# Nine edits of stage borders in a two-layer diffusion block on one core

## The chip, the cores and the metric

The kernel runs on one core of one Trainium2 chip. The metric is the device time of one execution in microseconds, taken as the median of several runs. An execution has one time of its own, and its profile has a span, from the first to the last instruction.

## The reference

Two transformer layers over 1024 latent tokens and 256 context tokens of width 1024, all in float32. Each layer is attention, an output projection, a layer norm, a gated feed-forward network with a 3-wide convolution, and a second layer norm. A conditioning vector gives shift, scale and gate for each half ("modulation").

```python
for i in range(2):
    sh1, sc1, g1, sh2, sc2, g2 = adaln(c, w_ada, b_ada)          # 6 x 1024 for the tokens
    csh1, csc1, cg1, csh2, csc2, cg2 = adaln(c_ctx, w_ada, b_ada)  # the same for the context
    h, hc = x * (1 + sc1) + sh1, xc * (1 + csc1) + csh1
    y, yc = mixer_i(h, hc)                    # attention, then @ w_out (1024 x 1024)
    x = layer_norm(ALPHA * x + g1 * y, ln1_g, ln1_b)
    h = x * (1 + sc2) + sh2
    x = layer_norm(ALPHA * x + g2 * conv_ffn(h), ln2_g, ln2_b)   # up: 1024 x 5632, down: 2816 x 1024
    # layer 0 does the same to the context; layer 1 has no use for it after the mixer,
    # so of its context modulation only csh1 and csc1 are read
return x
```

## The kernel before

Every float32 operand of a product is split in a high and a low part (`split_hi`, a cast; `split_lo`, a subtraction), and a product is three matmuls (`three`). Any of VectorE (DVE), ScalarE (ACT) and GpSimd (POOL) can do a split; the code says which. Tokens are worked on in chunks: chunk 0 and 1 are 512 tokens each, chunk 2 the 256 of the context. Activations lie feature-major, so a layer norm transposes on TensorE (PE), norms the rows and transposes back.

The tail of a layer (`layer_tail`) has these stages in program order:

- **Projection** (`proj`): eight output blocks of 128 features, first for chunk 0 (layer 0: chunks 0 and 2), then again for chunk 1. `load_wo` loads one 512 KB block of `w_out` and splits it on POOL, with the low part of odd blocks on DVE. The two first blocks are loaded ahead; each later one in its own turn. The steps of the first layer norm (`ln1`) of chunks 2 and 0 are woven in the second pass.
- **LN1 of chunk 1** (`ln1(1)`): four tiles of 128 tokens through `normalise`, eight feature blocks through `back_rows`, and then 20 operand tiles of the Strassen-like up product (sums of quarters, each split). The first products of the up stage (`HEAD` = 2 feature blocks in layer 0, 3 in layer 1; P1 and P2 of each) need chunk 0 alone and run between.
- **Up** (`up_step`): 22 feature blocks of seven products. In layer 0 one step of `next_modulation` follows each product: a DVE multiply-add over `w_ada` of layer 1. A piece (`ada_piece`) is eight such steps, four 512 KB loads, a split and a pair of matmuls.
- **Down** (`down_items`): three or four groups of feature-block pairs, seven products each; weights and activations are split as they come.
- **End**: layer 0 goes on to `layer1_head` (second layer norm, the latent projections, then per head group `up_q` and `up_kv`); layer 1 to `finish` (the last products per chunk, the last layer norm, the output).

Attention has a hand-written order with due times. Around it the Tile framework orders the instructions of each engine by program order and readiness, and a tile waits for a free slot of its tag. DMAs are issued in order on the SP queue, a few on POOL's (the first head of layer 1's attention, L2240) and ACT's. Slots of layer 0's tail: 7 of 2 KB ("r"), 32 of 2 KB ("b"), 11 of 4 KB ("c4", where `w_out` raw and split, the rows `z`, `x` and `w_ada` all go); layer 1: 8, 36, 12. PSUM has eight banks; the P1 bank of a feature block stays open until its P4.

Of the kernel before, what the change touches and what calls it, by code (L numbers as in the profile page):

```python
# [392 lines left out]
def tile_hybrid_block(ctx: ExitStack, tc: tile.TileContext, *aps):  # L393
# [182 lines left out]

    def ada_finish(l, ps, first=16, ends=(48, 48)):

        nc.tensor.transpose(ps[:, 0:96], arow, ident[0:96, 0:96])
        for c in range(2):  # L580
            a, b = first, ends[c]
            if a == b:
                continue
            nc.vector.tensor_add(
                mods[l][:, c, a:b], ps[:, 48 * c + a : 48 * c + b], vec_a[:, 16 + 48 * l + a : 16 + 48 * l + b]
            )
            for i in (1, 4):
                if a <= 8 * i < b:
                    nc.vector.tensor_scalar(mod(l, c, i), mod(l, c, i), 1.0, None, op0=ALU.add)

# [661 lines left out]
    def layer_tail(l, after, kept=None):  # L1252
# [48 lines left out]

        wo = []

        def load_wo(ci, m):
            first = ci == 0 and m == 0
            wo.append(
                load_w(
                    cols(A[f"l{l}_w_out"][:, m * P : (m + 1) * P]), f"o{l}_{ci}_{m}",
                    eng=("act" if first else "pool", "dve" if m % 2 or first else "pool"),
                )  # L1310
            )

        def proj(cis):
            for m in range(KB):
                if not wo:
                    load_wo(cis[0], m)
                wh, wl = wo.pop(0)
                for ci in cis:
                    c0, cn = chunks[ci]
                    yh, yl = ytiles[ci]  # L1320
                    ps = ps1(f"pso{l}_{ci}_{m}")
                    mm_acc(
                        ps[:, :cn],
                        [p3 for k in range(KB) for p3 in three(wh[:, k, :], wl[:, k, :], yh[:, k, :], yl[:, k, :])],
                    )
                    gate = mod(l, ci // 2, 2, m)
                    if l == 0:
                        nc.scalar.activation(acc[ci][:, m, :], ps[:, :cn], AF.Copy, scale=gate)
                    else:
                        xr = tl("xr", (512,), f"xr{l}_{ci}_{m}")  # L1330
                        nc.sync.dma_start(xr[:, :cn], x2_scr[m * P : (m + 1) * P, c0 : c0 + cn])
                        nc.vector.scalar_tensor_tensor(
                            acc[ci][:, m, :], ps[:, :cn], gate, xr[:, :cn], op0=ALU.mult, op1=ALU.add
                        )
                yield

        def normaliser(acc, pool, tl, ps1):
            def normalise(ci, j, name, residual=None, tag="c5", later=None):
# [19 lines left out]
                if later is not None:  # L1358
                    later.append((mv, rs))
                elif j % 2:  # L1360
                    nc.vector.tensor_scalar(rs[:, 1:2], mv[:, 0:1], rs[:, 0:1], -1.0, op0=ALU.mult, op1=ALU.mult)
                    nc.scalar.activation(z, z, AF.Identity, bias=rs[:, 1:2], scale=rs[:, 0:1])
                else:
                    nc.vector.tensor_scalar(z, z, mv[:, 0:1], rs[:, 0:1], op0=ALU.subtract, op1=ALU.mult)
# [4 lines left out]
        def back_rows(ci, zs, name, scales, residual, tl, ps1, order=range(KB)):  # L1369
# [3 lines left out]
            for m in order:  # L1373
                pb = ps1(f"pb{name}_{ci}_{m}")
                for j, z in enumerate(zs):
                    nc.tensor.transpose(pb[:, j * P : (j + 1) * P], z[:, m * P : (m + 1) * P], ident)
                tmp = tl("aa", (512,), f"tmp{name}_{ci}_{m}")[:, :cn]
                nc.vector.tensor_scalar(
                    tmp, pb[:, :cn], scales[0][:, m : m + 1], scales[1][:, m : m + 1], op0=ALU.mult, op1=ALU.add,
                )  # L1380
                if residual is not None:
                    residual(m, pb[:, :cn])
                yield m, tmp
# [67 lines left out]

        HEAD = 2 if l == 0 else 3
        lo, hi = slice(0, 512), slice(512, 1024)
# [131 lines left out]
        def next_modulation():  # L1585

            late = None
            for q, c in [(q, c) for c in range(2) for q in range(4)]:
                sums, rows = ada_piece(1, q, (c,), ps1, tl)
# [7 lines left out]
            run(late)  # L1597
            ada_finish(1, ps1("ps_af1"), 0, (16, 16))


        GROUPS = [(0, 1), (2, 3, 4), (5, 6, 7), (8, 9)] if l == 0 else [(0, 1, 2), (3, 4, 5, 6), (7, 8, 9)]
        def down_items():
# [31 lines left out]
            for i, (gi, js, what) in enumerate(steps):  # L1634
# [15 lines left out]
                if what != "A21":  # L1650
                    for j in js:
                        r = got.pop((i, j))
                        xh, xl = (tl("b", (512,), f"a{what}{s}_{l}_{j}", F32R) for s in "hl")
                        split_hi(xh, r, "act")
                        split_lo(xl, r, xh, "dve" if what in ("P1", "P3") else "pool")
                        xs.append((xh, xl))
# [59 lines left out]
        for m in range(2):  # L1716
            load_wo(0, m)
        if l == 0:
# [13 lines left out]
        for i in range(2 * HEAD):  # L1732
            step()
            for _ in range(4):
                next(rows, None)
# [151 lines left out]
        def back(ci, zs, name, scales, dst, residual):  # L1887
            for m, h in back_rows(ci, zs, name, scales, residual, tl, ps1):
# [6 lines left out]
             "feature_tile": feature_tile, "normalise": normaliser(acc, AC, tl, ps1), "back": back,  # L1895
             "load_w": load_w, "last_down": last_down,
             "tl_ada": lambda tag, shape, name, dt=F32: tlT("c4" if tag == "aw" else "r", shape, name, dt)}
        after(K)
# [6 lines left out]
    def layer1_head(K):  # L1905
# [96 lines left out]
        def rotate(x, tok, n, name):  # L2002
# [186 lines left out]
        run(norms[1])  # L2189
        def rest_of_modulation():  # L2190
            late = iter(())
            for q in range(4, 12):
                sums, rows = ada_piece(1, q, (0,), ps1, K["tl_ada"])
                for _ in sums:
                    next(late, None)
                    yield
                run(late)
                late = rows
            run(late)
            ada_finish(1, ps1("ps_af1"), 16, (48, 16))  # L2200

        mods_late = rest_of_modulation()

        def also(steps, n):
            for x in steps:
                for _ in range(n):
                    next(mods_late, None)
                yield x
# [54 lines left out]
    def finish(K):  # L2263
# [106 lines left out]
```

## Time and profile before

| | |
|---|---|
| median of 3 runs | 3573.13 us (3570.94 to 3577.04) |
| the profiled execution | 3575.87 us |
| its span | 3574.1 us |
| mean granted clock of PE | 0.965 |
| busy | PE 93%, weight loads 79%, DVE 68%, ACT 48%, POOL 44% |

The profiled execution's time is 1.8 us above its span and 2.7 us above the median. PE is the busiest engine; where it is idle, time is lost if the PE work behind it can't be made up.

### The profile page before, as it was taken

To read this page: it belongs to the slowest core of one execution; us is meant where nothing else is said; L and a number is where in the kernel's file an instruction comes from. 1 tells how busy PE (TensorE), PEld (TensorE's weight loads), DVE (VectorE), ACT (ScalarE), POOL (GpSimd) and SP (SyncE) were. 2 spreads that over 40 slices of the span, in tenths; PEclk is the share of its full clock that TensorE was granted. 3 is DMA by queue.
4 is the path that set the end of the run, shared out by engine and by line. 5 is a ranking of instruction groups with operands and counts; after the bars stand their busy time and mean duration, and the time that the engine had idled before them with its cause. 6 is when DMAs were issued, how large, how long until landed. Compare 5 with 4: busy or idle time off the path is not lost.

```text
span 3574.1 us, 52193 instructions
## 1 busy us (share of the span) xinstructions
PE 3307.3 (93%) x18683; PEld 2836.0 (79%) x18683; DVE 2447.3 (68%) x3777; ACT 1709.7 (48%) x3255; POOL 1584.3 (44%) x1794
## 2 busy tenths in 40 slices
PE   7998898988789999999999987999999889999997
PEld 5988787877668888888877776999998768888775
DVE  6687787873598766675655764777775387777665
ACT  4222677762354433443335323777775254444342
POOL 4533787652300000057734522888887300000985
PEclk9999999999899999999999988999999999999998
DMA  6367411574344422263323588232333323334541
GB/s 213 113 206 217 112 44 45 160 190 135 124 133 156 141 86 88 77 230 113 98 73 105 178 304 252 53 82 64 81 75 90 106 96 104 98 109 144 189 133 71
DMA packets 383744, 454.50 MB, mean 127 GB/s; under 512 B 27956, under 2 KB 255196, under 8 KB 383484
## 3 DMA queue, kind: packets, MB, share of 16 engines
q1 hardware_dynamic: 370284, 424.55, 39.2%
q10 hardware_dynamic: 11424, 18.94, 1.5%
q0 software_dynamic: 1776, 7.67, 0.6%
q8 instruction: 147, 2.41, 0.3%
q14 instruction: 113, 0.93, 0.1%
HBM read 328.78 MB, written 122.22 MB: 126 GB/s over the span
## 4 chain that ended last, share of the span: by engine, by line
PE 70%; DVE 9%; POOL 9%; issue 5%; DMA 3%; ACT 2%; SPq 0%; ACTq 0%; POOLq 0%; DVEq 0%
PE pu L1448 22%; PE pd_P L1778 10%; PE psum L194 7%; PE psum L335 5%; PE pso L417 5%; PE psum L304 5%; PE px L1522 3%; POOL p L264 3%; PE pw L417 2%; PE psq L417 2%; PE px L1778 2%; PE ps_f L417 2%; DVE aa L552 2%; PE ps_tu L417 1%; POOL pl L312 1%
## 5 line engine op out<-in xcount | busy, mean ns | idle before, releaser
L194 PE MATMUL psum<-k,q 96*128 96x512 f32 (+1 forms) x1152 | 272.8, 374 | 15.1 <-DMA k<-kr_scr 12.4
L412 POOL TENSOR_TENSOR dP<-dr,dP 128x512 fp32r<-128x512 f32 x40 | 57.0, 1445 | 454.2 <-ACT dP L404 450.5
L194 PEld LDWEIGHTS psum<-k,q 96*128 96x128 f32 x1152 | 196.8, 192 | 43.8 <-issue 12.8
L264 POOL TENSOR_SCALAR p_m<-p_m,st_m 128x640 f32<-128x640 f32 x256 | 202.6, 804 | 12.6
L552 DVE SCALAR_TENSOR_TENSOR aa<-aw,silu_late,aa 128x512 f32<-128x512 f32 x224 | 196.1, 905 | 15.4 <-DMA aw<-in_l_w_ada_dram 13.9
L320 DVE TENSOR_TENSOR pl_m<-psum,ph_m 128x512 fp32r<-128x512 f32 x256 | 175.0, 684 | 38.0 <-ACT ph_m L314 37.0
L304 PE MATMUL psum<-ident,p_m 128*128 128x128 f32 x1280 | 193.1, 273 | 2.5 <-DVE pl_m L320 2.2
L251 ACT ACTIVATE p_m<-psum,st_m 128x1024 f32<-128x1024 f32 (+2 forms) x192 | 187.0, 984 | 17.3 <-DVE st_m L244 16.4
L314 ACT CAST ph_m<-psum 128x512 fp32r<-128x512 f32 x256 | 151.0, 591 | 87.5 <-PE psum L304 44.1
L412 POOL TENSOR_TENSOR aal<-aa,aah 128x512 fp32r<-128x512 f32 x32 | 50.3, 1583 | 307.5 <-ACT aah L404 282.5
L412 POOL TENSOR_TENSOR aP2l<-ar_P,aP2h 128x512 fp32r<-128x512 f32 x20 | 28.7, 1450 | 354.0 <-ACT aP2h L404 346.9
L1770 DVE SCALAR_TENSOR_TENSOR acd<-pd_P,mods,acd 128x512 f32<-128x512 f32 x196 | 140.4, 742 | 54.9 <-PE pd_P L1778 49.9
L335 PE MATMUL psum<-ph_m,v 128*128 128x256 f32 x640 | 175.3, 301 | 0.6 <-DVE y_m L353 0.6
L335 PE MATMUL psum<-ph,v 128*128 128x256 f32 (+1 forms) x512 | 150.2, 316 | 23.0 <-DVE y L368 11.9
L241 DVE TENSOR_REDUCE st_m<-psum 128x1 f32<-128x1024 f32 (+1 forms) x128 | 105.6, 825 | 88.5 <-PE psum L194 88.5
L320 DVE TENSOR_TENSOR pl<-psum,ph 128x512 fp32r<-128x512 f32 (+1 forms) x224 | 144.7, 647 | 30.6 <-ACT ph L314 27.5
L335 PE MATMUL psum<-pl_m,v 128*128 128x256 f32 x640 | 164.1, 282 | 0.0
L304 PE MATMUL psum<-ident,p 128*128 128x128 f32 x960 | 151.7, 278 | 10.5 <-ACT p_c L118 4.3
L264 POOL TENSOR_SCALAR p<-p,st 128x640 f32<-128x640 f32 x192 | 152.9, 805 | 12.6
L314 ACT CAST ph<-psum 128x512 fp32r<-128x512 f32 (+1 forms) x224 | 122.9, 557 | 66.3 <-PE psum L304 59.3
L304 PEld LDWEIGHTS psum<-ident,p_m 128*128 128x128 f32 x1280 | 149.0, 141 | 4.0 <-DVE pl_m L320 3.1
L304 PEld LDWEIGHTS psum<-ident,p 128*128 128x128 f32 x960 | 110.3, 141 | 29.0 <-DVE pl L320 8.0
(599 smaller groups left out, 11406.5 us busy)
## 6 DMA issues: line engine op xcount, KB each, us to landing
aw<-in_l_w_ada_dram SPq DMA_DIRECT2D x96, 512.0 KB
ur<-in_l_w_up_dram SPq DMA_DIRECT2D x176, 256.0 KB
ar_P<-a_scr SPq DMA_DIRECT2D x140, 256.0 KB
a_scr<-a_t SPq DMA_DIRECT2D x80, 256.0 KB
dr<-in_l_w_down_dram SPq DMA_DIRECT2D x80, 256.0 KB
fr_o<-in_l_w_out_dram SPq DMA_DIRECT2D x32, 512.0 KB
a_scr<-cv SPq DMA_DIRECT2D x60, 256.0 KB
v<-v_scr SPq DMA_DIRECT2D x17, 640.0 KB
```

Source lines behind the costliest of these rows:

```text
L194: nc.tensor.matmul(u["s"][bank][:, c:e], q[:, qc], ks, start=pi == 0, stop=pi == len(u["passes"]) - 1)
L251: nc.scalar.activation(pt, src if bias is None else pt, AF.Exp, bias=st[:, j, 2:3], scale=1.0 if bias is None else -1.0, accum_out=st[:, j ...
L264: nc.gpsimd.tensor_scalar(pt, pt, st[:, j, 7:8], 0.0, op0=ALU.mult, op1=ALU.add)
L304: nc.tensor.transpose(tp[:, off + bi * P : off + bi * P + P], pts[j][:, c : c + P], ident)
L314: nc.scalar.copy(ph[:, :w], tp[:, :w])
L320: nc.vector.tensor_tensor(pl[:, :w], tps[g][:, :w], ph[:, :w].bitcast(F32), ALU.subtract)
L335: nc.tensor.matmul(u["av"][:, q0 : q0 + bw], u["v"][:, kt, :], m[:, off : off + bw], start=first and part == 0, stop=last and part == 1, s ...
L417: nc.tensor.matmul(ps, s, m, start=i == 0, stop=i == n - 1)
L552: nc.vector.scalar_tensor_tensor(accs[c], w, sck, accs[c], op0=ALU.mult, op1=ALU.add)
L1448: nc.tensor.matmul(ps, st, mv, start=start and i == 0, stop=i == len(pairs) - 1, skip_group_check=True)
L1770: nc.vector.scalar_tensor_tensor(acc[ci][:, m, :], src, mod(l, ci // 2, 5, m), acc[ci][:, m, :], op0=ALU.mult, op1=ALU.add)
L1778: nc.tensor.matmul(ps, st, mv, start=start and i == 0, stop=i == len(pairs) - 1, skip_group_check=True)
```

## The change

Nine edits:

1. `load_wo` loads a block in two 256 KB halves (tag "r"), two blocks ahead of its use through both passes; high parts on ACT, low parts on DVE, except that in the second pass the first half's go to POOL.
2. In LN1 of chunk 1 (both layers) all four tiles are normed on ACT, and `back_rows` makes its scaled copy on ACT.
3. `HEAD` of layer 1 is 4 rather than 3, with three steps of `ln1(1)` after each product rather than four.
4. The whole of layer 1's modulation (16 pieces) is made in the up stage of layer 0. Before, 8 pieces were made there and 8 in `layer1_head` (`rest_of_modulation`).
5. In `down_items` the low parts of odd pairs' activations go to DVE.
6. The pool of the first head of layer 1's attention (`pf`) is opened before that of the other heads (`pk`), so it lies at another address.
7. `finish` does chunk 1 in halves of 256 tokens.
8. The rotation's temporary takes a slot of "acc512".
9. The order of the last head group's `up_q` and `up_kv` is "bbbabaa" rather than "bbababa".

```diff
-        def load_wo(ci, m):
-            first = ci == 0 and m == 0
-            wo.append(
-                load_w(
-                    cols(A[f"l{l}_w_out"][:, m * P : (m + 1) * P]), f"o{l}_{ci}_{m}",
-                    eng=("act" if first else "pool", "dve" if m % 2 or first else "pool"),
-                )
-            )
+        out_blocks = iter([(p, m) for p in range(2) for m in range(KB)])
+
+        def load_wo():
+            p, m = next(out_blocks, (None, None))
+            if p is None:
+                return
+            wh, wl = (tl("fw", (KB, P), f"fo{s}{l}_{p}_{m}", F32R) for s in "hl")
+            for half in range(2):
+                ks = slice(4 * half, 4 * half + 4)
+                raw = tl("r", (4, P), f"ro{l}_{p}_{m}_{half}")
+                nc.sync.dma_start(
+                    raw,
+                    A[f"l{l}_w_out"][half * 512 : half * 512 + 512, m * P : (m + 1) * P].rearrange("(k p) c -> p k c", p=P),
+                )
+                split_hi(wh[:, ks], raw, "act")
+                split_lo(wl[:, ks], raw, wh[:, ks], "dve" if p == 0 or half else "pool")
+            wo.append((wh, wl))
...
-                if not wo:
-                    load_wo(cis[0], m)
                 wh, wl = wo.pop(0)
+                load_wo()
...
-                elif j % 2:
+                elif j % 2 or ci == 1 and name[0] == "a":
                     nc.vector.tensor_scalar(rs[:, 1:2], mv[:, 0:1], rs[:, 0:1], -1.0, op0=ALU.mult, op1=ALU.mult)
                     nc.scalar.activation(z, z, AF.Identity, bias=rs[:, 1:2], scale=rs[:, 0:1])
...
+                if ci == 1 and name[0] == "a":
+                    nc.scalar.activation(
+                        tmp, pb[:, :cn], AF.Identity, bias=scales[1][:, m : m + 1], scale=scales[0][:, m : m + 1]
+                    )
+                else:
...
-        HEAD = 2 if l == 0 else 3
+        HEAD = 2 if l == 0 else 4
...
-            for q, c in [(q, c) for c in range(2) for q in range(4)]:
+            for q, c in [(q % 12, q // 12) for q in range(16)]:
...
-                        split_lo(xl, r, xh, "dve" if what in ("P1", "P3") else "pool")
+                        split_lo(xl, r, xh, "dve" if what in ("P1", "P3") or j % 2 else "pool")
...
-            for _ in range(4):
+            for _ in range(4 if l == 0 else 3):
                 next(rows, None)
...
-            t = tl("aa", (512,), f"rt_{name}")[:n]
+            t = T.tile([P, 512], F32, name=f"rt_{name}", tag="acc512", bufs=16)[:n]
...
-        weave(also(up_q(0), 4), also(kv, 4), "")
+        weave(up_q(0), kv, "")
         for g in range(1, 4):
-            weave(also(up_q(g), 3), also(up_kv(g), 3), "babababa" if g < 3 else "bbababa")
-        run(mods_late)
+            weave(up_q(g), up_kv(g), "babababa" if g < 3 else "bbbabaa")
...
+        pf = es.enter_context(wait_pool("att1f", "right"))
         pk = es.enter_context(wait_pool("att1k", "right"))
-        pf = es.enter_context(wait_pool("att1f", "right"))
...
-        for ci, o, n in ((0, 0, 512), (1, 0, 512)):
+        for ci, o, n in ((0, 0, 512), (1, 0, 256), (1, 256, 256)):
```

`ada_finish` is fitted to the pieces' new place and does the same additions.

## Rows read from the trace of the kernel before

**Rows 1.** Windows: busy us (instructions) of each engine, PE clock, DMA share, GB/s.

```profile
887.40:971.40 84.00, 59.74 (x265) 46.91 (x264) 44.31 (x73) 26.04 (x45) 26.60 (x23) 0.80 0.34 105
...
971.40:1023.10 51.70, 34.87 (x198) 28.52 (x196) 46.96 (x83) 25.59 (x41) 3.47 (x5) 0.89 0.23 84
...
1030.00:1182.00 152.00, 152.00 (x798) 128.41 (x796) 132.36 (x194) 69.84 (x115) 11.13 (x6) 1.00 0.55 173
...
1182.00:1260.00 78.00, 76.35 (x402) 64.37 (x401) 54.33 (x84) 31.69 (x53) 4.69 (x2) 1.00 0.34 105
...
1260.00:1445.00 185.00, 185.00 (x976) 157.56 (x976) 117.31 (x175) 74.09 (x121) 0.00 (x0) 1.00 0.27 88
...
2054.00:2199.00 145.00, 128.82 (x633) 107.93 (x634) 92.14 (x143) 45.47 (x96) 38.39 (x44) 0.91 0.80 283
...
2757.00:2857.00 100.00, 87.80 (x389) 71.26 (x389) 39.31 (x56) 18.78 (x30) 39.84 (x28) 0.91 0.41 122
...
2868.00:2909.30 41.30, 29.32 (x128) 21.66 (x128) 39.42 (x67) 26.30 (x43) 1.92 (x2) 0.92 0.26 86
...
3305.00:3340.00 35.00, 27.24 (x108) 21.28 (x107) 21.24 (x21) 14.29 (x25) 35.00 (x24) 0.85 0.47 149
...
3551.70:3574.10 22.40, 4.30 (x30) 2.94 (x28) 18.06 (x24) 6.70 (x10) 10.42 (x6) 0.72 0.23 94
```

**Rows 2.** Waits in 887.4 to 971.4: us in total, times, longest.

```profile
PE pso L417 <- POOL fh_o L408: 15.6, 3, 7.6
...
PE pba L1376 <- DVE za L1364: 6.1, 2, 3.2
```

**Rows 3.** Chain of work that ended last: start us, us, what.

```profile
906.78 5.63 PE pso L417 x24
...
957.36 1.31 PE pba L1376 x12
...
1050.00 2.73 PE pu L1448 x12
...
2186.82 0.46 PE ps_a L417 x2
```

**Rows 4.** Timeline of layer 1's LN1 of chunk 1, ACT and DVE.

```profile
2868.46 0.62 ACT L404 CAST wP<-ur_00h 128x512 fp32r<-128x512 f32 x1
...
2868.98 1.25 ACT L1362 ACTIVATE za<-za,rs_a 128x1024 f32<-128x1024 f32 x1
...
2869.93 0.68 DVE L412 TENSOR_TENSOR wP<-ur_00h,wP 128x512 fp32r<-128x512 f32 x1
...
2873.03 0.81 DVE L1378 TENSOR_SCALAR tmpa<-pba,der 128x512 f32<-128x512 f32 x1 [1.16 <-PE pba L1376]
...
2873.88 0.78 ACT L1408 ACTIVATE rs<-pba,der 128x512 f32<-128x512 f32 x1 [1.27 <-DVE tmpa L1378]
```

**Rows 5.** Waits of PE in 2800 to 2910.

```profile
PE pso L417 <- POOL fh_o L408: 10.5, 2, 5.3
```

**Rows 6.** Tile aa and aal: min/median/max ns, first and last start.

```profile
L552 DVE SCALAR_TENSOR_TENSOR aa<-aw,silu_late,aa x224: 732/745/1831, 206.2 to 2180.4; 128x512 f32<-128x512 f32 x112
...
L412 POOL TENSOR_TENSOR aal<-aa,aah x32: 1267/1372/3400, 229.0 to 2181.9; 128x512 fp32r<-128x512 f32 x32
```

**Rows 7.** Waits of PE in 2070 to 2230.

```profile
PE psum L194 <- DMA k<-kr_scr: 12.4, 1, 12.4
...
PE psq L417 <- ACT uqh L404: 11.0, 1, 11.0
```

**Rows 8.** POOL's timeline where layer 1's attention begins.

```profile
2199.04 0.70 POOL L2240 DMA_DIRECT2D q<-q_scr  x1 [11.85 <-PE psq L417]
```

**Rows 9.** Waits of PE in 3305 to 3515.

```profile
PE pd_P L1778 <- POOL aP6l L412: 11.3, 5, 6.5
```

**Rows 10.** Groups by line in 3305 to 3515: count, busy us, mean ns, idle before.

```profile
L412 POOL TENSOR_TENSOR aP6l<-ar_P,aP6h 128x512 fp32r<-128x512 f32 x10 | 14.8, 1497 | 0.1
...
L412 DVE TENSOR_TENSOR aP3l<-ar_P,aP3h 128x512 fp32r<-128x512 f32 x10 | 13.4, 1360 | 2.7 <-ACT aP3h L404 2.4 <-issue 0.3
```

More of the change, by code (lines that the diff above doesn't have):

```diff
@@ L575, in ada_piece, with ada_finish @@
         return column_sums(), rows()
-    def ada_finish(l, ps, first=16, ends=(48, 48)):
+    def ada_finish(l, ps):
+        lo = 16 if l == 0 else 0
         nc.tensor.transpose(ps[:, 0:96], arow, ident[0:96, 0:96])
         for c in range(2):
-            a, b = first, ends[c]
-            if a == b:
-                continue
+            hi = 16 if (l == 1 and c == 1) else 48
             nc.vector.tensor_add(
-                mods[l][:, c, a:b], ps[:, 48 * c + a : 48 * c + b], vec_a[:, 16 + 48 * l + a : 16 + 48 * l + b]
+                mods[l][:, c, lo:hi], ps[:, 48 * c + lo : 48 * c + hi], vec_a[:, 16 + 48 * l + lo : 16 + 48 * l + hi]
             )
-            for i in (1, 4):
-                if a <= 8 * i < b:
-                    nc.vector.tensor_scalar(mod(l, c, i), mod(l, c, i), 1.0, None, op0=ALU.add)
+            if l == 1:
+                nc.vector.tensor_scalar(mod(l, c, 1), mod(l, c, 1), 1.0, None, op0=ALU.add)
+            if l == 0 or c == 0:
+                nc.vector.tensor_scalar(mod(l, c, 4), mod(l, c, 4), 1.0, None, op0=ALU.add)
     def chunk_of(t):
@@ L1377, in back_rows @@
                 tmp = tl("aa", (512,), f"tmp{name}_{ci}_{m}")[:, :cn]
-                nc.vector.tensor_scalar(
-                    tmp, pb[:, :cn], scales[0][:, m : m + 1], scales[1][:, m : m + 1], op0=ALU.mult, op1=ALU.add,
-                )
+                if ci == 1 and name[0] == "a":
[3 more added lines that the diff above has]
+                else:
+                    nc.vector.tensor_scalar(
+                        tmp, pb[:, :cn], scales[0][:, m : m + 1], scales[1][:, m : m + 1], op0=ALU.mult, op1=ALU.add,
+                    )
                 if residual is not None:
@@ L1597, in next_modulation @@
             run(late)
-            ada_finish(1, ps1("ps_af1"), 0, (16, 16))
+            ada_finish(1, ps1("ps_af1"))
         GROUPS = [(0, 1), (2, 3, 4), (5, 6, 7), (8, 9)] if l == 0 else [(0, 1, 2), (3, 4, 5, 6), (7, 8, 9)]
@@ L1716, in layer_tail @@
         for m in range(2):
-            load_wo(0, m)
+            load_wo()
         if l == 0:
@@ L1895, in layer_tail @@
              "feature_tile": feature_tile, "normalise": normaliser(acc, AC, tl, ps1), "back": back,
-             "load_w": load_w, "last_down": last_down,
-             "tl_ada": lambda tag, shape, name, dt=F32: tlT("c4" if tag == "aw" else "r", shape, name, dt)}
+             "load_w": load_w, "last_down": last_down}
         after(K)
@@ L2189, in layer1_head @@
         run(norms[1])
[L2190 to L2208, printed above, removed]
-        weave(also(up_q(0), 4), also(kv, 4), "")
+        weave(up_q(0), kv, "")
         for g in range(1, 4):
-            weave(also(up_q(g), 3), also(up_kv(g), 3), "babababa" if g < 3 else "bbababa")
-        run(mods_late)
+            weave(up_q(g), up_kv(g), "babababa" if g < 3 else "bbbabaa")
     layer_tail(0, layer1_head)
```

## Prediction

> **What bounds the kernel now.** I read the page first: PE is busy 93% of the span, so the question is where the other 7%, and the time at a low clock, lie. The tenths of the page show PE full in the attentions and the up and down stages, and gaps between them. So I cut the span at the stages with the windows [rows 1] and read there who PE waits for. The reader is to see three kinds of stretch. First, stretches in which PE never stops: the two parts of the up stage of layer 0 at 1030 and 1260 have PE busy for all of their 152 and 185 us at full clock [rows 1]; there only PE work counts. Second, stretches in which PE waits for weights: the second projection pass of layer 0 (887 to 971) has PE busy 59.7 of 84 us at a mean granted clock of 0.80, so some of it at the lower level, 1.2 GHz [rows 1], and the waits name POOL's high part of `w_out` for 15.6 us [rows 2]; layer 1's is alike, 87.8 of 100 us [rows 1] and 10.5 us [rows 5]. Third, stretches in which DVE is full and PE hungry: LN1 of chunk 1, DVE 47.0 of 51.7 us in layer 0 and 39.4 of 41.3 us in layer 1 [rows 1]. The chain gives prices of PE work [rows 3].
>
> **The change part by part**, against the profiled execution (3575.87 us, span 3574.1).
>
> *w_out in halves, two blocks ahead.* In the layer 0 stretch PE needs 8 blocks of 5.63 us and 96 transposes (6 token tiles x 8 in, 8 x 2 and 8 x 4 out) of 1.31/12 = 0.11 us [rows 3]: 45.0 + 10.5 = 55.5 us. The stretch takes 84, so at most 28.5 us can go. The named wait for POOL is 15.6, and the 6.1 for `za` [rows 2] falls partly too, since PE then has the next block to run while the rows are normed. I take 18; the lower end is 0, if another wait steps in. What is late next is the norm of chunk 0, on DVE: 44.3 us of work [rows 1] in some 66. In layer 1 idle is 12.2 us and the clock 0.91 [rows 1]; I take 10, bounds 0 and 21 (idle, and 9 us if all of the lost clock were given back). The new splits cost ACT 2 x 0.62 and DVE 1 or 2 x 0.68 us a block [rows 4], under a block's 5.6 us of PE: hidden. SP issues 64 loads rather than 32; if a half lands late, two blocks (11 us) stand between it and PE. Slots: three blocks in flight hold 6 of 11 "c4"; four `z` and one `x` fit beside them, exactly.
>
> *ACT in LN1 of chunk 1.* DVE loses 8 copies of 0.81 us [rows 4] and two norms, which I price like such a copy, and gains two scalars of one column, which I leave out: 6.5 + 1.6 = 8.1 us. ACT gains 8 x 0.78 + 2 x 1.25 = 8.7 [rows 4], and has 25.6 busy of 51.7 [rows 1]: room. Layer 0: 7 us, bounds 0 (ACT late instead) and 8.1. In layer 1 the fourth `HEAD` block adds two low parts and one addition on DVE, 3 x 0.68 = 2.0, and brings PE 2 x 2.73 = 5.5 us of products [rows 3] that the up stage then need not do: 8.1 - 2.0 + 5.5 = 11.6, capped by PE's idle time there, 41.3 - 29.3 = 12.0 [rows 1]. I take 8; bounds 0 and 12.
>
> *Modulation back in the up stage.* Moved are 8 pieces: 32 loads on SP, 8 x (7 x 0.745 + about 0.5) = 46 us of DVE [rows 6], 8 casts, 8 POOL subtractions, 8 pairs of matmuls of 0.46 us [rows 3] and 8 small DMAs on ACT's queue. Where they go PE never stops, so the pairs cost 8 x 0.46 = 3.7 us. DVE hides the rest if it has room: in 1260 to 1445 it is busy 117.3 of 185 (63%); a piece takes 5.7 us in the 25 us of a feature block, 23% more; the sum, 86%, is what 1030 to 1182 shows with the pieces in (132.4 of 152, 87%), and PE is full there [rows 1]. I take 4 lost; worse bound 10, with a wait like the 1.65 us of 1182 to 1260 [rows 1] for each two of the 8 pieces, 6.6 more. Where they leave (2054 to 2199) PE's idle is 16.2 us with the DMA engines 80% busy [rows 1]; 11.0 of it waits for split weights of `up_q` [rows 7], whose loads queue on SP behind `w_ada` loads that wait for slots. I take 13 gained: 3.7 of pairs and most of the 11. Bounds 3.7 and 20.
>
> *First head's pool.* PE waits 12.4 us for the first key [rows 7], since POOL's loads wait for a tile that the last `psq` reads [rows 8]. At the new address lie the slots of `layer1_head`'s tables and low parts, some of which the last `psq` reads too. Nothing shows which; 3 us, bounds 0 and 10.
>
> *Odd pairs on DVE.* Layer 1's down stage loses 11.3 us to POOL's P6 low parts [rows 9], most of it in 3305 to 3340, where POOL is busy all 35 us [rows 1]. Two of the POOL operations ahead of the last P6 part go to DVE, 2 x 1.5 = 3.0 us [rows 10]; with layer 0 I take 4, bounds -3 (DVE late) and 11.
> The row shows DVE paying for POOL: its subtraction takes 1.36 us there [rows 10] and 0.68 where POOL rests [rows 4]. The Trainium skill (SBUF — State Buffer, Who interferes with whom) says that a DVE operation with two SBUF inputs and GpSimd hold the same port pair in turn, so the loser waits out the whole instruction; the trace agrees with a price twice as high. By that rule the move frees the pair of 1.5 - 0.68 us an operation and not of 1.5, and this part would give 2 rather than 4.
>
> *End in halves.* After the last products DVE works 18.1 us of 22.4 [rows 1] for four tiles; with two left that is 9 less at best. The first half's work must fit before. I take 5, bounds -2 and 9.
>
> *The temporary and the order of the last group* move no work: 0, under PE's products.
>
> Sum: 18 + 10 + 7 + 8 + 13 + 3 + 4 + 5 - 4 = 64 us. 3575.9 - 64 = 3511.9; the profiled execution lies 2.7 above the median, so 3509, told as 3510.
>
> **The rivals.** (a) *Half of it is given back* as other waits: the slots of "c4" are just enough, and if `z` and `x` take them first, the two-block lead is one block and the projections give little (28 lost at worst), and the uq loads may be late by themselves (9 lost). For it: SP issues in order, behind stores that wait for ACT. Against: raw `w_out` no longer takes "c4". Half of 64 is 32: 3541. (b) *All of it*, clock included: near their upper ends the first four terms and the head give 28 + 15 + 8 + 12 + 20 = 83; with 17 for the pool, the down stage and the end, less 4, that is 96: 3477. For it: waits and low clock stand in the same stretches [rows 1]. (c) *No change*: the new stages keep PE's idle time and only rename what it waits for; 3573. Against it: the pairs of matmuls and DVE's 8.1 us are certain. (d) *Slower*: in the up stage PE stops once in each of 16 pieces for the row products, as long as the longest POOL subtraction, 3.4 us [rows 6], which is 54 us, and the clock falls to 0.91 as at 2757 [rows 1] over 16 x 25 = 400 us, 36 us more. 54 + 36 + 4 less the 68 of the other terms is +26: 3600. It decides once a stop costs over 68/16 = 4.3 us a piece. Against it: 8 pieces ran there with 1.65 us of idle PE in all. (e) *The port pair decides in the down stage*: by the rows, if a DVE subtraction always costs 1.36 us there, DVE gets 25 x 1.36 = 34 us more a layer and hands POOL's wait to DVE's evictions; that part then gives 0 instead of 4, and the sum is 60: 3514. The Trainium skill's rule on that pair, named above, is this rival. I give it one in two; it lies inside every case.
>
> **How the numbers follow.** A measurement of this kernel tells 0.2%, 7 us, from no change. Forecast (3490 to 3530): 0.57. (a) 3530 to 3558: 0.22. (b) 3455 to 3490: 0.11. (c): 0.04. (d) and slower cases: 0.06. The likeliest is 3510. The range from 3475 to 3555 leaves out some 5% below and some 13% above. Faster 0.57 + 0.22 + 0.11 = 0.90, same 0.04, slower 0.06.
>
> **What would show it.** Projections: no PE wait for `w_out`, a stretch of some 66 us where 84 stood, the clock near 1. LN1 of chunk 1: DVE's work some 8 us less, PE's restart as much earlier. Up stage: 3.7 us longer, PE still full, DVE near 87% for 16 pieces. Head: no wait of 11 us for `uqh`, DMA share well under 0.80. The first head's loads: who POOL waits for at its first load. Wrong it would be if new waits of PE for ACT stood in the projections, or idle PE at the `ps_a` products.

## The result: 3521.9 us, and the profile after

The changed kernel takes 3521.88 us (median; 3520.65 to 3523.39) and the kernel before 3575.09 us beside it (3570.94 to 3577.09): a ratio of 0.9853, interval 0.9836 to 0.987. The forecast was 3510 us, range 3475 to 3555, and faster. The profiled execution of the changed kernel spans 3521.1 us, 53.0 less than before.

To see where these 53 us lie, I cut both spans at the start of a stage's first or last product (tiles `pso`, `pu`, `pd_P`, `px`, `psk`, `psq` in the trace; the up stage, for one, runs from the first to the last P3). Every number of the table is a difference of two such starts, each rounded to 0.1 us; the gains add up to the 53.0.

| stage (us) | before | after | gained | predicted |
|---|---|---|---|---|
| start to second projection pass, layer 0 | 881.9 | 884.8 | -2.9 | 0 |
| second projection pass, layer 0 | 93.0 | 69.7 | 23.3 | 18 |
| LN1 of chunk 1, layer 0 (first P1 to first P3) | 58.8 | 54.6 | 4.2 | 7 |
| up stage, layer 0 | 523.8 | 527.1 | -3.3 | -4 |
| down stage, layer 0 | 257.7 | 258.8 | -1.1 | 4 with layer 1's |
| its end, LN2 | 188.4 | 187.1 | 1.3 | 0 |
| head of layer 1 | 196.1 | 177.7 | 18.4 | 13 |
| first head's load and attention 1 | 545.1 | 544.9 | 0.2 | 3 |
| first projection pass, layer 1 | 46.8 | 46.4 | 0.4 | 0 |
| second projection pass, layer 1 | 73.3 | 59.2 | 14.1 | 10 |
| LN1 of chunk 1 and up stage, layer 1 | 441.6 | 445.2 | -3.6 | 8 |
| down stage, layer 1 | 208.1 | 205.5 | 2.6 | see layer 0 |
| end | 59.5 | 60.1 | -0.6 | 5 |

The first row looks untouched and is not: the first projection pass lies in it, and `load_wo` serves that pass too. The pass took 72.9 us before (71.8 in e1 below, which loads as before) and 68.4 to 70.3 in the changed kernel and all other variants. In front of it the edit costs as much again. The `w_out` halves loaded ahead (`ro`) wait 22.0 us on SP for PE's `psum` (L304), and the loads of attention's output (`yr`) stand behind them in the same queue. So from attention's last eviction (`avt`) to the first split of `y_0h` it takes 3.7 us before, 4.5 in e1, and 7.4 to 8.9 in all others. SP's timeline, before and then after:

```profile
802.50 16.47 SPq L1294 DMA_DIRECT2D yr<-y_scr  x12
```

```profile
804.69 3.15 SPq L1312 DMA_DIRECT2D ro<-in_l_w_out_dram  x6
807.95 11.82 SPq L1293 DMA_DIRECT2D yr<-y_scr  x9
```

From the last `avt` to the second pass it is 77.2 us in both kernels. The 2.9 us lost are attention's own end, 804.7 and 807.6 us, which no edit touches.

The windows of the changed kernel answer to [rows 1] (us; then busy time of PE, PEld, DVE, ACT, POOL with counts, granted clock, DMA share, GB/s):

```profile
884.80:954.50 69.70, 62.17 (x323) 51.14 (x321) 44.13 (x79) 32.20 (x57) 17.63 (x18) 0.95 0.44 140
954.50:998.30 43.80, 31.08 (x165) 24.70 (x165) 36.61 (x69) 30.32 (x49) 3.46 (x5) 0.91 0.24 85
1009.10:1160.00 150.90, 150.90 (x792) 127.77 (x791) 131.22 (x192) 68.40 (x111) 11.12 (x6) 1.00 0.55 171
1236.00:1420.00 184.00, 183.23 (x966) 155.02 (x965) 150.57 (x224) 79.34 (x130) 11.31 (x7) 1.00 0.50 158
2029.00:2160.00 131.00, 124.79 (x624) 106.46 (x624) 52.33 (x96) 39.37 (x83) 23.57 (x32) 0.95 0.61 219
2751.10:2810.30 59.20, 56.28 (x289) 47.26 (x288) 33.58 (x55) 27.03 (x46) 14.91 (x13) 0.97 0.40 125
2813.00:2858.00 45.00, 34.88 (x155) 27.08 (x153) 35.64 (x64) 34.75 (x56) 1.10 (x2) 0.92 0.28 92
2882.30:2902.30 20.00, 15.76 (x62) 12.38 (x60) 14.90 (x22) 7.25 (x13) 0.00 (x0) 0.91 0.36 118
```

The kernel before over its two second passes, from the first `pso` product to the first P1:

```profile
881.87:974.87 93.00, 68.74 (x323) 54.84 (x321) 47.77 (x78) 28.36 (x48) 27.56 (x24) 0.82 0.36 112
2791.60:2864.95 73.35, 61.27 (x290) 49.99 (x288) 34.16 (x54) 21.60 (x36) 23.90 (x18) 0.88 0.32 97
```

Line by line: the second projection pass of layer 0 now has PE busy 62 of 70 us at a clock of 0.95; before, 69 of 93 us at 0.82 (0.80 in the shorter window of [rows 1]). The up stage of layer 0 is full with all 16 pieces in it, DVE 82 to 87%. The head's DMA share is 0.61. In layer 1's LN1 (2813 to 2858) ACT is as busy as DVE, 34.75 and 35.64 of 45 us, and at 2882, in the up stage, there is a 20 us stretch with PE idle for 4.2, which the kernel before did not have.

Waits of PE in the second projection pass of layer 0 (us in total, times, longest), beside [rows 2]: no wait for `w_out` is left.

```profile
PE pba L1382 <- DVE za L1370: 5.2, 2, 4.1
PE pba L1382 <- ACT za L1368: 2.0, 1, 2.0
```

ACT's timeline in layer 1's LN1 of chunk 1 (start, us), the counterpart of [rows 4]; behind it DVE's of the same stretch:

```profile
2813.55 4.64 ACT L1368 ACTIVATE za<-za,rs_a 128x1024 f32<-128x1024 f32 x4 [1.95 <-DVE rs_a L1367]
...
2818.76 0.78 ACT L1385 ACTIVATE tmpa<-pba,der 128x512 f32<-128x512 f32 x1
2819.43 0.77 ACT L1419 ACTIVATE rs<-pba,der 128x512 f32<-128x512 f32 x1
2820.09 0.78 ACT L1385 ACTIVATE tmpa<-pba,der 128x512 f32<-128x512 f32 x1
2820.76 0.79 ACT L1419 ACTIVATE rs<-pba,der 128x512 f32<-128x512 f32 x1
```

```profile
2819.28 0.69 DVE L1542 TENSOR_TENSOR g<-pu,g 128x512 f32<-128x512 f32 x1 [3.42 <-PE pu L1459]
...
2820.90 0.69 DVE L1451 TENSOR_TENSOR tmpa<-tmpa,tmpa 128x512 f32<-128x512 f32 x1 [0.33 <-ACT tmpa L1385]
2822.24 0.69 DVE L1451 TENSOR_TENSOR tmpa<-tmpa,tmpa 128x512 f32<-128x512 f32 x1 [0.65 <-ACT tmpa L1385]
```

ACT does four norms, then for each row block a `tmp` and a residual in turn, some 1.33 us a block; DVE, the engine that was to be relieved, stands idle for `tmp`, 2.9 us in all over five of the eight.

Waits in the new stop at 2882 to 2902 (all engines):

```profile
ACT wP L404 <- DVE s L1212: 4.5, 1, 4.5
PE pu L1459 <- ACT wP L404: 4.2, 1, 4.2
```

POOL's timeline at layer 1's first head, beside [rows 8]: `q` no longer waits, but `k`, issued behind it, waits for the same last `psq`.

```profile
2151.66 0.70 POOL L2229 DMA_DIRECT2D q<-q_scr  x1 [0.65 <-POOL qev L2017]
...
2160.77 0.58 POOL L2229 DMA_DIRECT2D k<-k_scr  x1 [7.84 <-PE psq L417]
```

Waits of PE from the down stage of layer 1 to the end, beside [rows 9]:

```profile
PE pd_P L1789 <- POOL aP6l L412: 9.9, 2, 7.6
PE ptc L1351 <- DVE acd L1896: 7.8, 2, 4.6
```

### The profile page after: what moved, and what is told of

Read it like the earlier page. It is cut to its first block, busy times and chain, and to the rows that moved or that the text cites. A ratio compares the mean times of both kernels' runs of the same rounds, so it can differ in the third digit from the quotient of the medians.

```text
span 3521.1 us, 52490 instructions
## 1 busy us (share of the span) xinstructions
PE 3291.1 (93%) x18730; PEld 2834.5 (81%) x18730; DVE 2480.9 (70%) x3850; ACT 1755.3 (50%) x3335; POOL 1461.3 (42%) x1714
## 4 chain that ended last, share of the span: by engine, by line
PE 42%; DVE 4%; POOL 3%; ACT 2%; issue 2%; DMA 2%; SPq 0%; POOLq 0%; ACTq 0%; DVEq 0%
PE pu L1459 10%; PE pd_P L1789 8%; PE psum L194 6%; PE psum L335 4%; PE psum L304 4%; PE pw L417 2%; PE psq L417 2%; PE pso L417 2%; PE px L1789 1%; PE pl L417 1%; PE psk L417 1%; PE psv L417 0%; POOL dr L1216 0%; DMA k<-kr_scr 0%; DMA dr<-in_l_w_down_dram 0%
## 5 line engine op out<-in xcount | busy, mean ns | idle before, releaser
L194 PE MATMUL psum<-k,q 96*128 96x512 f32 (+1 forms) x1152 | 273.1, 374 | 13.8 <-DMA k<-kr_scr 11.2
L412 POOL TENSOR_TENSOR aal<-aa,aah 128x512 fp32r<-128x512 f32 x32 | 50.7, 1595 | 447.5 <-ACT aah L404 372.6
L264 POOL TENSOR_SCALAR p_m<-p_m,st_m 128x640 f32<-128x640 f32 x256 | 201.8, 801 | 12.6
L320 DVE TENSOR_TENSOR pl_m<-psum,ph_m 128x512 fp32r<-128x512 f32 x256 | 174.8, 684 | 37.4 <-ACT ph_m L314 36.4
L304 PE MATMUL psum<-ident,p_m 128*128 128x128 f32 x1280 | 193.3, 274 | 2.5 <-DVE pl_m L320 2.2
L552 DVE SCALAR_TENSOR_TENSOR aa<-aw,silu_late,aa 128x512 f32<-128x512 f32 x224 | 186.7, 862 | 8.1 <-DMA aw<-in_l_w_ada_dram 7.4
L304 PE MATMUL psum<-ident,p 128*128 128x128 f32 x960 | 151.9, 278 | 10.4 <-ACT p_c L118 4.2
L264 POOL TENSOR_SCALAR p<-p,st 128x640 f32<-128x640 f32 x192 | 152.3, 801 | 12.6
L304 PEld LDWEIGHTS psum<-ident,p_m 128*128 128x128 f32 x1280 | 149.0, 141 | 3.7 <-DVE pl_m L320 3.1
L304 PEld LDWEIGHTS psum<-ident,p 128*128 128x128 f32 x960 | 110.5, 142 | 28.9 <-DVE pl L320 8.2
L335 PE MATMUL psum<-pl,v 128*128 128x256 f32 (+1 forms) x512 | 132.5, 282 | 0.0
```

The source lines that it names most:

```text
L194: nc.tensor.matmul(u["s"][bank][:, c:e], q[:, qc], ks, start=pi == 0, stop=pi == len(u["passes"]) - 1)
L264: nc.gpsimd.tensor_scalar(pt, pt, st[:, j, 7:8], 0.0, op0=ALU.mult, op1=ALU.add)
L304: nc.tensor.transpose(tp[:, off + bi * P : off + bi * P + P], pts[j][:, c : c + P], ident)
L320: nc.vector.tensor_tensor(pl[:, :w], tps[g][:, :w], ph[:, :w].bitcast(F32), ALU.subtract)
L335: nc.tensor.matmul(u["av"][:, q0 : q0 + bw], u["v"][:, kt, :], m[:, off : off + bw], start=first and part == 0, stop=last and part == 1, s ...
L552: nc.vector.scalar_tensor_tensor(accs[c], w, sck, accs[c], op0=ALU.mult, op1=ALU.add)
```

## The experiments

Each kernel was timed in three rounds beside the kernel before; the ratio is to that. Code that no edit touches varies between the profiled executions (attention 0 ended at 803 to 813 us, attention 1 with the first load took 542 to 546), so the length of the edited stage carries the verdict on a small part, and the time only supports it. Kernels with the same code in a stage agree within 0.6 us in layer 1's down stage and end, 1.3 in the second passes and layer 0's up stage, 1.9 in the LN1 stretches and layer 0's down stage, and 2.8 in the head; a difference below that is not told from none.

**e1: `w_out` as before.**

```
-        def load_wo():          # halves, two blocks ahead, ACT and DVE
...
+        def load_wo(ci, m):     # whole, one block, POOL and every second low part DVE
...
```

> The changed kernel with w_out loaded whole and late again, split on POOL and DVE as before; the rest of the change stays. Theory A (PE's wait for the split weights is what the two projections gained; the stages add): the anchors of the two second passes moved by 23.3 and 13.8 us, so the time is 36 us above the changed kernel, 3558 us (3552 to 3564), PE waits for the high part from POOL for some 15 us in layer 0 and 10 us in layer 1, and the granted clock of the layer 0 pass is back near 0.80. Rival B (PE's wait only moves on, and part of the gain at the anchors is lost again in LN1 of chunk 1 behind it, which is bound by DVE): 15 to 25 us above, some 3541, with LN1 of chunk 1 quicker by the difference.

Measured 3552.3 us, ratio 0.9947 (0.9927 to 0.9968). The two second passes took 92.4 and 72.6 us: 22.7 and 13.4 more than in the changed kernel, 36.1 together. Waits of PE, layer 0's pass, then layer 1's:

```profile
PE pso L417 <- POOL fh_o L408: 15.9, 3, 7.6
```

```profile
PE pso L417 <- POOL fh_o L408: 10.5, 2, 5.3
```

The windows of the two passes:

```profile
883.00:975.40 92.40, 67.88 (x321) 54.39 (x320) 47.75 (x78) 28.33 (x48) 27.47 (x24) 0.83 0.35 114
2766.70:2839.30 72.60, 60.51 (x288) 49.47 (x287) 34.32 (x54) 21.53 (x36) 23.76 (x18) 0.88 0.32 98
```

LN1 of chunk 1 in layer 0 took 53.8 us against 54.6, in layer 1 with the up stage 445.7 against 445.2: nothing worth the name is given back. Theory A holds, with the time, 30.4 us above the changed kernel, at the low end of its range. The span is only 29.7 longer, since the start, the head and attention 1 were 1.8, 1.8 and 2.9 shorter in that execution; the edit touches the start alone, where its two effects cancel, as said above.

**e2: the modulation pieces back in the head.**

```
-            for q, c in [(q % 12, q // 12) for q in range(16)]:
+            for q, c in [(q, c) for c in range(2) for q in range(4)]:
...
-            weave(up_q(g), up_kv(g), "babababa" if g < 3 else "bbbabaa")
+            weave(also(up_q(g), 3), also(up_kv(g), 3), "babababa" if g < 3 else "bbababa")
...
```

> The changed kernel with the 8 modulation pieces of condition 0 back in the head of layer 1, as before; the rest of the change stays. Theory A: the head gained 18.4 us and the up stage of layer 0 lost 3.6, so the time is 15 us above the changed kernel, 3537 us (3533 to 3541), the up stage is 3.6 us shorter, and PE waits some 11 us for the split weights of up_q. Rival B (the head's gain came from the earlier down stage and from the moved rotation temporary, not from the pieces): within 5 us of the changed kernel, 3517 to 3527.

This also puts the last group's order (edit 9) back. Measured 3548.5 us, ratio 0.9932 (0.9913 to 0.995). The head took 201.9 us, 24.2 more (175.0 to 177.8 in the kernels with the new head); the up stage of layer 0 took 522.5, 4.6 less: 19.6 net by the stages, 26.6 by the medians. Waits of PE in the head, and a window of it:

```profile
PE psq L417 <- ACT uqh L404: 11.8, 2, 8.3
```

```profile
2029.00:2181.00 152.00, 128.86 (x637) 105.62 (x637) 91.09 (x145) 46.73 (x99) 37.37 (x44) 0.96 0.75 269
```

Theory A's mechanism holds and its size was low: with the pieces PE waits for the split `up_q` weights as in [rows 7], and the DMA share is 0.75. How much of the 24.2 is the order's was not tried. This head is also 5.8 us longer than the one before (196.1), with the rotation's temporary (edit 8) as the only edit left in it: PE's busy time is the same (173.5 and 173.7 us), its idle time 28.4 against 22.5. Whether edit 8 costs that was not tried either.

**e3, e4, e8: layer 1's LN1.** e3 takes ACT out of it, e4 takes the fourth `HEAD` block out, e8 both.

```
-                elif j % 2 or ci == 1 and name[0] == "a":
+                elif j % 2 or ci == 1 and name[:2] == "a0":      # e3, e8; the same for tmp
...
-        HEAD = 2 if l == 0 else 4
+        HEAD = 2 if l == 0 else 3                                # e4, e8
-            for _ in range(4 if l == 0 else 3):
+            for _ in range(4 if l == 0 else 4):                  # e4, e8
```

> The changed kernel with ACT's norms and scalings in LN1 of chunk 1 for layer 0 alone; in layer 1 the normed rows and the scaled temporaries go back to DVE, HEAD stays 4. Theory A (in layer 1 ACT took over the bound: four norms in a row, then a temporary and a residual for each block of rows, 34.8 of 45 us busy, and DVE waits for each): LN1 of chunk 1 in layer 1 is 4 to 8 us shorter, 3514 to 3518 us. Rival B (DVE needs what ACT took; the loss lies in the fourth HEAD block): 3 to 8 us longer, 3525 to 3530. Rival C (both engines are as late): 3520 to 3524.

> The changed kernel with three HEAD blocks in layer 1 and four rows of LN1 behind each step, as before; ACT's part stays. Theory A (ACT is the bound in that LN1, and the fourth block only fills a wait): LN1 ends at the same time, the block's 5.5 us of products come after it, 3522 to 3528 us. Rival B (the fourth block's weights, split on ACT and DVE, delay the rows, so that it costs more than its 5.5 us of products give): 3513 to 3519 us.

> The changed kernel with layer 1's LN1 of chunk 1 as before: three HEAD blocks, four rows behind each step, norms and scalings of layer 1 on DVE; layer 0 keeps ACT. Theory A (both halves of that edit lose in layer 1: ACT's share 1.2 us, the fourth block 2.4 us): the stretch from the first P1 product to the last P3 product of layer 1 takes 441.6 us as before, and the time is 3 to 4 us below the changed kernel, 3517 to 3519. Rival B (with the quicker projection the old form is worse than it was, since the norms of chunk 0 are not done): the stretch takes 445 or more, 3522 or above.

| | time, ratio | LN1 (P1 to P3) | up stage, layer 1 | down stage, layer 1 |
|---|---|---|---|---|
| before | 3575.09 | 49.3 | 392.3 | 208.1 |
| changed | 3521.88, 0.9853 | 52.0 | 393.2 | 205.5 |
| e3 | 3520.28, 0.986 (0.9838 to 0.9882) | 50.7 | 393.2 | 205.5 |
| e4 | 3516.67, 0.9843 (0.9827 to 0.986) | 50.5 | 392.3 | 203.4 |
| e8 | 3513.89, 0.9831 (0.9817 to 0.9846) | 49.8 | 392.3 | 203.7 |

The fourth block brings 5.5 us of products forward, so the up stage behind it should be 5.5 shorter; it is 0.9 longer. The windows of e4 (first) and e3 (second) for the place of the stop show why:

```profile
2879.70:2899.70 20.00, 20.00 (x90) 16.58 (x89) 18.62 (x27) 10.51 (x17) 0.00 (x0) 1.00 0.36 118
```

```profile
2877.50:2897.50 20.00, 15.76 (x62) 12.34 (x61) 14.89 (x22) 7.24 (x13) 0.00 (x0) 0.91 0.36 118
```

With four blocks PE stops for 4.2 us, with or without ACT; with three it doesn't. The stop also takes the clock down to 0.91 in this window: 62 matmuls take 15.76 us, 0.25 each, where with three blocks 90 take 20.00, 0.22 each. That is some 2 us more, and the stop and the clock together (6.2) outweigh the 5.5. What makes DVE late is read from the timelines, not tried: feature blocks whose P1 and P2 are already done leave PE five products, 13.7 us by [rows 3], while DVE still has all their weight sums and the activations to do, and waits in order for PE and ACT between them; a third such block in a row runs out of lead. In e3 the expectation of 4 to 8 us (Theory A) fell: the LN1 is 1.3 us shorter (up to 2.5 against the other kernels with the changed LN1, 52.0 to 53.1), and the time is Rival C's. In e4 Rival B holds for the block, though not by delayed rows but by the later stop; its LN1 is 1.5 shorter only because 5.5 us of products left it. In e8 the stretch took 442.0 us, 441.6 before: Theory A. By the medians e8 gains 8.0 us where Theory A had 3 to 4; the stretch gives 3.2, and by the profiles the start and attention 1, which the edit does not touch, were 3.8 and 2.4 us shorter. With three blocks the down stage of layer 1 is 2 us shorter too, but the end behind it is 1.2 longer (61.2 in e4 and 61.3 in e8, 60.1 in the changed kernel and e3): 0.6 to 1.0 us are left, which I can't place.

**e5: the first head's pool.**

```
-        pf = es.enter_context(wait_pool("att1f", "right"))
         pk = es.enter_context(wait_pool("att1k", "right"))
+        pf = es.enter_context(wait_pool("att1f", "right"))
```

> The changed kernel with the first head's pool of layer 1 back where it was (pk opened ahead of pf); the rest stays. Theory A (the new address lets the q loads go some 9 us early, but the k load, issued behind them, still waits 7.8 us for the last psq): the k and q loads both wait, PE's wait for the first key stays at 11 to 13 us, and the time is 0 to 2 us above the changed kernel, 3521 to 3524. Rival B (the prediction's 3 us): 3525, with PE's wait 3 us longer.

Measured 3523.02 us, ratio 0.9855 (0.9838 to 0.9871). Waits of POOL, then of PE:

```profile
POOL q L2229 <- PE psq L417: 9.3, 1, 9.3
```

```profile
PE psum L194 <- DMA k<-kr_scr: 12.6, 1, 12.6
```

PE's wait is 12.6 us, 11.2 in the changed kernel: 1.4 us between these two. But in the kernels that keep the new address and the new head the wait is 9.9 to 12.7 us, so a gain from the address is not shown. What is shown is Theory A's mechanism: at the old address `q` waits 9.3 us for the last `psq`, and at the new one `k` does, 7.8.

**e6: odd pairs back on POOL.**

```
-                        split_lo(xl, r, xh, "dve" if what in ("P1", "P3") or j % 2 else "pool")
+                        split_lo(xl, r, xh, "dve" if what in ("P1", "P3") else "pool")
```

> The changed kernel with the low parts of odd j in the down stages back on POOL, in both layers; the rest stays. Theory A (the port pair: DVE pays for what POOL is spared): the down stage of layer 0 is 1 us shorter, that of layer 1 2 to 3 us longer with a wait of 11 us for P6's low part, in all 3522 to 3525 us. Rival B (4 us of the prediction, both layers): 3526. Rival C: the move costs as much as it gives, 3519 to 3522. DVE's two-input subtraction there costs 1.36 us with POOL busy, nearer 1.0 or less where POOL rests.

Measured 3526.69 us, ratio 0.9862 (0.9847 to 0.9876). Layer 1's down stage took 207.6 us, 2.1 more, and layer 0's 259.2, 0.4 more. The split of tile `aP6l` in layer 1 (min/median/max ns), changed kernel, then e6:

```profile
L412 POOL TENSOR_TENSOR aP6l<-ar_P,aP6h x5: 1297/1599/1724, 3268.2 to 3410.8; 128x512 fp32r<-128x512 f32 x5
L412 DVE TENSOR_TENSOR aP6l<-ar_P,aP6h x5: 846/1126/1769, 3271.2 to 3411.8; 128x512 fp32r<-128x512 f32 x5
```

```profile
L412 POOL TENSOR_TENSOR aP6l<-ar_P,aP6h x10: 1265/1452/1739, 3273.7 to 3421.6; 128x512 fp32r<-128x512 f32 x10
```

The edit is worth some 2 us in layer 1; the 0.4 of layer 0 lies within the variation of that stage (257.4 to 258.9 in the kernels with the edit). DVE pays 1.13 us (median) for a part and the five left on POOL cost 1.60 instead of 1.45. Theory A holds in layer 1; its loss of 1 us in layer 0 is not seen. The time itself is Rival B's, but of the 6.9 us by which the profile is longer 4.9 stand in front of layer 0's second pass, where the edit isn't.

**e7: the end in two chunks of 512.**

```
-        for ci, o, n in ((0, 0, 512), (1, 0, 256), (1, 256, 256)):
+        for ci, o, n in ((0, 0, 512), (1, 0, 512)):
```

> The changed kernel with the end in two chunks of 512, not 512, 256, 256; the rest stays. Theory A (the first half's norms ran no earlier, since PE waits in the end for DVE's gated sums, 7.8 us, so halving moved the wait): within 1.5 us of the changed kernel, 3520.5 to 3523.5, the end from the last row product of the down stage 0.6 us shorter. Rival B (the halves give the predicted 5 us, and something else lost them, such as the earlier down stage): 3526 to 3528.

Measured 3519.07 us, ratio 0.9844 (0.9829 to 0.9858). The end took 57.9 us against 60.1 with halves. The waits of PE there:

```profile
PE ptc L1351 <- DVE acd L1896: 2.9, 2, 2.6
PE pl L417 <- ACT pdt L1893: 2.8, 1, 2.8
```

Against 7.8 us for `acd` in the changed kernel: the halves lose 2.2 us, more than Theory A gave them. That PE has less work of the next chunk to run while DVE gates the sums of the last is read from these waits.

**e9 to e12: undoing what lost, and two steps further.** e9 is e8 with the end of e7. On top of it, e10 puts `tmp` on ACT for odd row blocks alone, with every second norm, in both layers; e11 has no ACT in either layer; e12 puts the first group's even low parts of layer 1's down stage on DVE too.

```
+                elif j % 2:                                                       # e10, e11
+                if ci == 1 and name[0] == "a" and m % 2:                          # e10
+                if False:                                                         # e11, in its place
+                        ... "dve" if what in ("P1", "P3") or j % 2 or l and gi == 0 else "pool"   # e12
```

> The changed kernel with the two losing parts taken back together: layer 1's LN1 of chunk 1 as before (three HEAD blocks, DVE) and the end in two chunks of 512. Theory A (the stages add: 4.5 us from LN1 and the up stage of layer 1, 2.3 us from the end): 6 to 7 us below the changed kernel, 3511 to 3516. Rival B (an earlier up stage only makes the down stage or the end wait longer): 3517 to 3520.

> As e9_best, but in both layers ACT takes the scaled temporaries of odd row blocks alone, and every second norm. Theory A (in the row phase whichever engine does all of it is the bound, and half and half is quicker than either): in layer 1 the stretch from the first P1 to the first P3 product takes 45 to 48 us rather than 49.8; in layer 0 that from P1 to P7 42 to 43 rather than 43.7; 2 to 5 us below e9_best. Rival B (the row phase isn't the bound in layer 1, the 50 operations of DVE behind it are, and these are as many): layer 1 within 1 us of 49.8, layer 0 slower (45 to 46).

> As e9_best, but without ACT's share in layer 0 either, so that LN1 of chunk 1 is as in the kernel before in both layers. Theory A (ACT's share is what shortened layer 0's stretch from P1 to P7 from 48.2 to 43.8 us): that stretch is back at 48, and the time 4 to 5 us above e9_best. Rival B (the quicker projection shortened it, by leaving less of chunk 0's work in it): 44 to 45, within 1 us of e9_best.

> As e9_best, but in the first group of layer 1's down stage all low parts of the activations are on DVE, even j too. Theory A (PE waits 7.6 us there for POOL's last low part of P6, which stands behind 13 POOL operations, while DVE has some 3 us of idle time in those 26): the wait falls to 0 to 4 us, 4 to 7 us below e9_best. Rival B (the port pair: DVE's own operations cost 1.1 to 1.7 us each beside POOL, so that PE waits for DVE's low parts instead): within 2 us of e9_best.

| | time, ratio | LN1, layer 0 (P1 to P7) | LN1, layer 1 (P1 to P3) | down and end, layer 1 |
|---|---|---|---|---|
| changed | 3521.88, 0.9853 | 43.8 | 52.0 | 265.6 |
| e9 | 3513.13, 0.9839 (0.9823 to 0.9856) | 43.6 | 49.8 | 262.4 |
| e10 | 3514.63, 0.984 (0.9826 to 0.9855) | 49.9 | 47.4 | 262.4 |
| e11 | 3520.83, 0.9855 (0.984 to 0.987) | 49.6 | 50.2 | 262.8 |
| e12 | 3510.59, 0.9832 (0.9817 to 0.9846) | 44.9 | 50.2 | 259.6 |

e9 spans 13.2 us less than the changed kernel (3507.9); 8.7 by the medians, somewhat above the 6 to 7 expected, and in the range given. e11 shows what ACT is worth in layer 0: 6.0 us against e9, 4.7 against e12, which has the same code there. e10 splits the two: in layer 1 half and half is quicker than either engine alone (47.4; ACT 50.5 in e4, DVE 49.8), as Theory A had it; in layer 0 it gives nothing, which Theory A had wrong, as it had the time (1.5 us above e9, not 2 to 5 below). There PE waits 10.8 us for split weights in e10 and in e11, in e9 6.5. The first `tmp` starts 15 us behind the first P1 product in e9 and 18 in e10. ACT's timeline, e10 and then e9:

```profile
956.82 1.24 ACT L1368 ACTIVATE za<-za,rs_a 128x1024 f32<-128x1024 f32 x1 [6.07 <-DVE rs_a L1367]
...
964.46 1.24 ACT L1368 ACTIVATE za<-za,rs_a 128x1024 f32<-128x1024 f32 x1 [5.93 <-DVE rs_a L1367]
```

```profile
956.95 2.44 ACT L1368 ACTIVATE za<-za,rs_a 128x1024 f32<-128x1024 f32 x2 [2.67 <-DVE rs_a L1367]
...
966.66 1.24 ACT L1368 ACTIVATE za<-za,rs_a 128x1024 f32<-128x1024 f32 x1 [2.05 <-DVE rs_a L1367]
```

In layer 0 DVE adds the residual to the rows before it takes their statistics, so a norm left to DVE stands in the way of the next row's. That the norms and not the scalings carry the gain there is read from these lines and not shown; norms alone on ACT were not tried.

In e12 PE's waits in the down stage are small and spread over both engines:

```profile
PE pd_P L1789 <- DVE aP5l L412: 2.4, 1, 2.4
PE pd_P L1789 <- POOL aP6l L412: 2.3, 1, 2.3
```

The down stage took 200.1 us, 203.7 in e9: 3.6 gained, 2.8 with the end behind it, a little under Theory A's 4 to 7. e12 has the lowest time, 3510.59 us; e8, e9 and e12 can't be told apart by their intervals. e12 with e10's layer 1 was not tried.

## Why the prediction was right, and which of its terms were not

It had the sign, the range and the main place: PE's waits and its lost clock stand in the same stretches, and an earlier split gives both back. The sum was 64 us and came out at 53; the terms were off on both sides.

- **`w_out`, 28 us: right in mechanism, low.** The second passes gained 37.4 us, 36.1 when undone alone. In layer 0, 22.7 to 23.3 against 18: the wait for POOL of 15.6 [rows 2] went whole, and PE's idle time fell by 16.7 us, near the 18. What the 18 left out is the clock: it rose from 0.82 to 0.95, and the same products took 6.6 us less. In layer 1 it is 9.2 of idle time and 5.0 of clock, against 10. The sum of PE's work in that part was also wrong: it charged the window of [rows 1] with eight blocks, 55.5 us, but the window starts after the first and has 169 `pso` matmuls, seven blocks of 24, so 49.9, and 34 us could go rather than 28.5. The first pass and its loads, which the sum took at nothing, gained some 4 us and lost as much. Rival (a), the lead lost to slots or loads, did not happen in the second passes.
- **ACT in layer 0, 7 us: right.** 4.7 to 6.0 by e11, 4.2 between the two profiles; the shorter pass may leave a little more of chunk 0 to this stretch (43.8 us against 43.0 in e1), but that is within the variation.
- **ACT and the fourth block in layer 1, 8 us: the step that failed.** The measured value is -3.6, and -3.2 by e8 (445.2 against 442.0 us). I subtracted 8.1 us from DVE and wrote "room" beside ACT from its share of busy time; but the operations moved stand in a chain, norm, `tmp`, residual on one engine, and DVE waits for it. They gave nothing: without them the stretch is 0.8 us (e8 against e4) to 1.3 us (e3) shorter, which is within the variation, and with half of them (e10) it is 2.4 shorter than with none. And I credited the fourth block with 5.5 us of products that the up stage "need not do", without asking what DVE then does in the up stage: it is late by 4.2 us three feature blocks on, the clock falls behind that, and the block loses 1.9 (e8 against e3) to 2.4 us (e4 against the changed kernel) in all.
- **Modulation, 13 less 4: low.** The pieces, with the last group's order, cost the head 24.2 and the up stage gave back 4.6 (e2); between the profiles 18.4 and 3.3. The up stage's price, 3.7 us of pairs with DVE under 87%, came as worked out, and rival (d) did not occur.
- **First head's pool, 3 us: at most 1.4, and not told from none.** The address freed `q`; `k` still waits for the last `psq`.
- **Odd pairs, 4 us: some 2 by e6.** The price was mis-sized: a low part moved from POOL costs DVE 1.13 us in place of the 0.68 of [rows 4], and POOL's own went from 1.45 to 1.60. The Trainium skill (SBUF — State Buffer, Who interferes with whom) says that a DVE operation with two SBUF inputs contends with a POOL operation that reads SBUF, under an exclusive lock; my estimate by that rule was 2. The trace agrees: the two take turns, as the last section shows. Rival (e), no gain at all, did not hold; I had called that rival the Trainium skill's rule, though by that rule I had worked out 2 and not 0.
- **End in halves, 5 us: wrong sign, -2.2.** I priced the tail that gets shorter and only noted that "the first half's work must fit before". It doesn't: PE waits 7.8 us for the gated sums, 2.9 when the end isn't halved.

Three terms booked at 16 us of gain (LN1 of layer 1, the end, the pool) came to a loss of 4.4 to 5.8 (-3.6 - 2.2, and 1.4 or nothing); the projections and the head, 9.4 and 5.4 us larger than booked, made up for most of that. That the sum came as near as 53 to 64 is in part luck of this kind.

## What to carry to other kernels

Price a move between engines by the chain it lands in, not by the busy share of the engine that takes it: a share says nothing on an engine that must alternate between what is moved and what it already did, and splitting the run by halves can beat both (layer 1) or give nothing (layer 0). Work brought forward into a gap also takes cover from what stood behind it; ask which engine then falls behind, and how many blocks later. Loads issued ahead also hold up what stands behind them in the same queue: look at what that is. And where an engine's slow weights starve PE, book the granted clock with the wait: it came back with it.

## What the hardware showed that was not expected

The granted clock of the projection pass went from 0.83 to 0.95 with nothing but the loads and splits of `w_out` changed (e1 against the changed kernel), so that PE's own busy time fell from 67.9 to 62.2 us for the same products.

DVE's and POOL's subtractions take turns by whole operations. In layer 1's down stage of the changed kernel the split of a 128x512 low part took DVE 0.68 us where POOL rested. Where it started in the middle of a POOL subtraction, it ended 0.55 us behind that one in 38 of 40 cases, so that it took up to 1.79 us; POOL's own low parts took 1.29 to 1.78. Here DVE waits for POOL's second `aP5l`, which ends at 3285.23, and POOL's `aP7l` then for DVE, which ends at 3285.78:

```profile
3281.80 3.43 POOL L412 TENSOR_TENSOR aP5l<-ar_P,aP5h 128x512 fp32r<-128x512 f32 x2
3284.01 1.77 DVE L412 TENSOR_TENSOR aP7l<-ar_P,aP7h 128x512 fp32r<-128x512 f32 x1
3285.19 1.74 POOL L412 TENSOR_TENSOR aP7l<-ar_P,aP7h 128x512 fp32r<-128x512 f32 x1
```

Attention 0, which no edit touches, ended between 803.0 and 813.0 us in the profiled executions, a spread as wide as most single parts of this change. With one profile of each kernel, it is open whether that lies in the kernel or in the execution.
